# A three-layer mixed model on one core: the instruction order laid out by the scheduler's timeline machine model instead of its plain one

## The chip, the cores and the metric

The kernel runs on one core of a Trainium2 chip. Its engines are TensorE (PE, with its weight loads shown as PEld), VectorE (DVE), ScalarE (ACT), GpSimd (POOL) and SyncE (SP), which issues the loads. The metric is the device time in microseconds from start to end of one execution.

## The reference

The input is one sequence of 256 tokens of width 1024. Two blocks follow each other. The first has two layers, each with a feed-forward part, a mixer of three kinds of heads, a cross attention over 256 memory tokens, and a second feed-forward part. The second block is one hybrid layer with attention, a two-way gated delta rule and a convolutional feed-forward part. Cut to what matters:

```python
for l in range(2):                                            # first block
    x = x + 0.5 * swiglu(rms_norm(x, ...), ffn1_w_in[l], ffn1_w_out[l])
    z = rms_norm(x, ...) @ mix_w_in[l]                        # fox | moba | rwkv7
    x = x + concat([fox_mixer(..), rwkv7_mixer(..), moba_mixer(..)]) @ mix_w_out[l]
    x = x + memory_cross_attention(rms_norm(x, ..), rms_norm(mem, ..), ...)
    x = x + 0.5 * swiglu(rms_norm(x, ...), ffn2_w_in[l], ffn2_w_out[l])
# rwkv7_mixer, per token:   sa = S @ -kk
#   S = S * w + outer(sa, kk * a) + outer(v, k);   y = S @ r
mod = silu(c) @ w_mod + b_mod                                 # second block
ak, av, qkv, db, da, aq, z, gate = split_cols(modulate(rms_norm_2(x), sh1, sc1) @ w_in)
attn = latent_attention(q_x, [k_c, k_x], [v_c, v_x])
# gated delta rule: S_t = a_t (I - beta_t k_t k_t^T) S_(t-1) + beta_t k_t v_t^T;  o_t = S_t^T q_t
x = x + g1 * merge_branches(attn, gdn_output(gdn_bidirectional(ctx, x), z), gate)
x = x + g2 * conv_ffn(modulate(rms_norm_2(x), sh2, sc2), w_up, ..., w_down)
return rms_norm_2(x, final_norm_w)
```

The recurrences of `rwkv7_mixer` and of the gated delta rule are the serial parts. The kernel computes both in chunks, with the inverse of a unit triangular matrix in each chunk.

## The kernel before

**GEMMs.** Every product with a weight matrix is done in three passes with the operands split in a high and a low part, xh·wh + xl·wh + xh·wl. `piece` loads 128 x 1024 weights (512 KB) into `raw` (L370, SP's queue, 4 buffers), ACT makes `wh` (L319, 3 buffers) and DVE makes `wl` from both (L322, 3 buffers). The matmuls are L346, the transposes L349. `gemm_tok` has 512 columns per matmul (`wh`, `wl` as the moving operand), `gemm_chan` 256 columns (`xTh`, `xTl` as the moving operand, or `wh` stationary).

**Chains.** The rwkv heads of each mixer (function `rwkv`) run in two groups of heads, `gi` 0 and 1, and the gated delta rule of block 2 (`gdn`) in four groups. Each group builds a triangular matrix (`rN` in the mixers, L1121 and L1130; `gN` in block 2) and calls `inverse`: 15 stream shuffles (L696), 15 steps of a product `iv_p` (L322) and a sum `iv_x` (L343) on DVE, then the mask product (`rW`, or `xv` and `iv_tz` in block 2), transposes on DVE (L715, L735) and small matmuls on PE (`iv_tz,rN`, `rW,iv_tz`, `iv_tz,gN`) that double the size of the inverted blocks from 8 to 64 or 128. Behind it come the scans over the chunks (`rvt,rG`, `rX,rW`, `rSB` in a mixer; `gS,gQD`, `gdl,kT` in block 2) and the evacuation into `ry`, `rzr` or `go`. In the cross attention `xq` is the query, `xP` the softmax numerator and `macc` the product of the modulation weights with the condition vector, done on DVE (L340) out of raw weight pieces and summed over partitions by 128 x 2 matmuls.

**Order.** The functions are Python generators. `run` steps a main generator and merges side work into it by times (`Side`, `START`, `PACE`, the numbers given to `yield`), which fixes the order in which the instructions are traced. The tile layer then schedules them: it takes the traced instructions of all engines, goes through them greedily on a model of the machine, and lays out one order for each engine and the semaphore waits between the engines. On the chip every engine takes its instructions in that order. SP issues the loads in order too, and a load into `raw` waits until the splits of the piece four before have read it.

```python
r = s.stage.tile([128, 1024], F32, name="raw", bufs=4)         # raw
s.nc.sync.dma_start(r[:, :n], src)
h = s.stage.tile([128, 1024], F32R, name="wh", bufs=3)         # piece
l = s.stage.tile([128, 1024], F32R, name="wl", bufs=3)
s.act(h[:, :n], r[:, :n])
s.sub(l[:, :n], r[:, :n], h[:, :n].bitcast(F32))
```

The scheduler is chosen where `kernel` opens the tile context (L2054); all instructions come from `body`.

## Time and profile before

| | |
|---|---|
| median of 3 runs | 2138.4 us (2137.61 to 2144.73) |
| the profiled execution | 2140.43 us, span 2138.6 us |
| mean granted TensorE clock | 0.967 |
| PE, DVE, ACT, POOL busy | 96%, 75%, 53%, 1% |
| moved by DMA | 317.18 MB, 148 GB/s in the mean |

The stages, as the timeline shows them: feed-forward 0 to 235 us, mixer 0 to 447, cross attention 0 to 505, two feed-forward parts with the context side of block 2 beside them to 1040, mixer 1 to 1250, cross attention 1 with the modulation beside it to 1310, feed-forward to 1500, block 2's delta rule and attention to 1830, and the rest of block 2 to the end.

The page lists busy time, slices of the span, queues, the chain of work that ended last and the costliest groups. A matmul's end is modelled, so two of them overlap in the list, and what PE needs for one is read from the distance between starts. [...]

### The profile page before, as it was taken

How to read it: one execution, taken by the hardware profiler on the slowest of the kernel's cores; microseconds unless marked ns; L12 is line 12 of the kernel's file. 1: busy time of each engine (PE TensorE's matmuls, PEld its weight loads, DVE VectorE, ACT ScalarE, POOL GpSimd, SP SyncE). 2: the span in 40 equal slices, each digit the busy share in tenths (PEclk: the TensorE clock that was granted, in tenths of full speed). 3: DMA queues.
4: the chain of work that ended last, by engine and by line, in shares of the span. 5: the costliest groups of instructions: out<-in, count | busy, mean ns of one | idle time of the engine just before them, and what ended most of it. 6: DMA issues, size and time to landing. Idle time of an engine off the chain costs nothing.

```text
span 2138.6 us, 37333 instructions
## 1 busy us (share of the span) xinstructions
PE 2049.2 (96%) x14344; PEld 1808.0 (85%) x14344; DVE 1603.7 (75%) x3832; ACT 1131.0 (53%) x2113; POOL 14.9 (1%) x16
## 2 busy tenths in 40 slices
PE   8999999999999999999999979999889999999998
PEld 8899887778989989898888758889678888878996
DVE  6888688477686959586688576777778787767985
ACT  6544555376455555454555455435545565546663
POOL 0000000000000000000000000000000000000000
PEclk9999999899999999999999889999978999999999
DMA  7777432154554545454432154776431123555664
GB/s 246 226 236 231 154 110 70 52 169 131 166 160 140 156 139 159 137 166 145 148 107 80 53 187 155 248 239 206 138 99 60 40 70 93 168 165 167 194 192 128
DMA packets 90571, 317.18 MB, mean 148 GB/s; under 512 B 10389, under 2 KB 12953, under 8 KB 90009
## 3 DMA queue, kind: packets, MB, share of 16 engines
q1 hardware_dynamic: 90392, 314.80, 46.7%
q8 instruction: 112, 1.84, 0.3%
q14 instruction: 67, 0.54, 0.1%
HBM read 313.72 MB, written 1.05 MB: 147 GB/s over the span
## 4 chain that ended last, share of the span: by engine, by line
PE 73%; DVE 16%; DMA 5%; ACT 4%; issue 2%; SPq 0%; DVEq 0%; ACTq 0%
PE b L346 69%; DVE wl L322 4%; DMA raw<-in_wmod_dram 4%; PE b L349 3%; ACT wh L319 1%; DVE iv_x L343 1%; DVE iv_tz L696 1%; DVE macc L340 1%; DVE iv_p L322 1%; DVE gcv L340 1%; ACT sq L319 1%; DVE sg L322 1%; ACT iv_c L319 0%; DVE sg L340 0%; DVE iv_tz L322 0%
## 5 line engine op out<-in xcount | busy, mean ns | idle before, releaser
L319 ACT ACTIVATE wh<-raw 128x1024 fp32r<-128x1024 f32 (+1 forms) x546 | 568.6, 1042 | 553.9 <-PE b L346 437.9
L322 DVE TENSOR_TENSOR wl<-raw,wh 128x1024 fp32r<-128x1024 f32 (+1 forms) x546 | 653.8, 1203 | 242.9 <-ACT wh L319 211.5
L346 PE MATMUL b<-xTh,wh 128*128 128x256 f32 x2200 | 626.8, 286 | 2.8 <-ACT xTh L319 2.4
L346 PE MATMUL b<-xTh,wl 128*128 128x256 f32 x2200 | 622.4, 283 | 7.3 <-DVE wl L322 5.8
L346 PE MATMUL b<-xTl,wh 128*128 128x256 f32 x2200 | 621.8, 283 | 0.2 <-DVE xTl L340 0.2
L346 PEld LDWEIGHTS b<-xTh,wl 128*128 128x128 f32 x2200 | 418.4, 190 | 10.9 <-DVE wl L322 7.7
L346 PEld LDWEIGHTS b<-xTh,wh 128*128 128x128 f32 x2200 | 417.2, 190 | 8.5 <-ACT xTh L319 4.4
L346 PEld LDWEIGHTS b<-xTl,wh 128*128 128x128 f32 x2200 | 418.4, 190 | 2.7 <-DVE xTl L340 0.8
L346 PE MATMUL b<-wh,gh 128*128 128x512 f32 x440 | 177.7, 404 | 2.4 <-DVE x L340 2.2
L346 PE MATMUL b<-wl,gh 128*128 128x512 f32 x440 | 174.4, 396 | 0.2 <-DVE wl L322 0.2
L346 PE MATMUL b<-wh,gl 128*128 128x512 f32 x440 | 174.0, 396 | 0.0
L346 PE MATMUL b<-wh,xTh 128*128 128x512 f32 x400 | 163.6, 414 | 6.4 <-DVE iv_x L343 5.0
L346 PE MATMUL b<-wl,xTh 128*128 128x512 f32 x400 | 164.2, 412 | 0.3 <-DVE wl L322 0.3
L346 PE MATMUL b<-wh,xTl 128*128 128x512 f32 x400 | 161.4, 404 | 0.0
L340 DVE SCALAR_TENSOR_TENSOR macc<-raw,mcs,macc 128x512 f32<-128x512 f32 x112 | 82.4, 746 | 31.9 <-DMA raw<-in_wmod_dram 31.6
L346 PEld LDWEIGHTS b<-wh,gh 128*128 128x128 f32 x440 | 83.7, 190 | 20.8 <-DVE x L340 2.9
L346 PEld LDWEIGHTS b<-wl,gh 128*128 128x128 f32 x440 | 83.7, 190 | 19.6 <-DVE wl L322 0.6
L346 PEld LDWEIGHTS b<-wh,xTh 128*128 128x128 f32 x400 | 76.4, 192 | 26.2 <-issue 9.1
L346 PEld LDWEIGHTS b<-wh,gl 128*128 128x128 f32 x440 | 83.8, 191 | 17.0
L346 PEld LDWEIGHTS b<-wl,xTh 128*128 128x128 f32 x400 | 76.5, 191 | 20.1 <-issue 3.7
L346 PEld LDWEIGHTS b<-wh,xTl 128*128 128x128 f32 x400 | 76.9, 192 | 15.5 <-issue 1.0
L319 ACT ACTIVATE iv_tz<-b 32x128 f32<-32x128 f32 (+2 forms) x96 | 31.1, 324 | 63.5 <-PE b L346 62.5
(608 smaller groups left out, 3189.7 us busy)
## 6 DMA issues: line engine op xcount, KB each, us to landing
raw<-in_f1i_dram SPq DMA_DIRECT2D x88, 512.0 KB, 4.4
raw<-in_f2i_dram SPq DMA_DIRECT2D x88, 512.0 KB, 3.8
raw<-in_wmod_dram SPq DMA_DIRECT2D x48, 512.0 KB, 4.3
raw<-in_wup_dram SPq DMA_DIRECT2D x44, 512.0 KB, 4.3
raw<-in_f1o_dram SPq DMA_DIRECT2D x40, 512.0 KB, 4.1
raw<-in_wi_q_dram SPq DMA_DIRECT2D x40, 512.0 KB, 3.8
raw<-in_f2o_dram SPq DMA_DIRECT2D x40, 512.0 KB, 4.0
raw<-in_wi_a_dram SPq DMA_DIRECT2D x32, 512.0 KB, 3.9
```

What stands on the lines that cost most here:

```text
L319: return s.nc.scalar.activation(out, in_, func, scale=scale, bias=bias, **kw)
L322: return s.nc.vector.tensor_tensor(out, a, b, op=op)
L340: return s.nc.vector.scalar_tensor_tensor(out, a, sc, b, op0=op0, op1=op1)
L343: s.nc.vector.tensor_reduce(out, in_, axis=AX.X, op=op)
L346: s.last_mm = s.nc.tensor.matmul(out, lhsT, rhs, start=start, stop=stop).ins
L349: s.nc.tensor.transpose(out, in_, s.c("ident"))
L696: nc.vector.stream_shuffle(AR[:, j, :, j:], NC[:, :, j:], [j] * 16 + [16 + j] * 16)
```

## The change

One argument is added. The scheduler then goes through the same traced instructions on its timeline model of the machine instead of the plain one. All instructions stay, by name and operands, but for two more ACT table loads (6 instead of 4); what changes is their order on each engine and, with it, the waits. The orders of PE (11000 rows before, 11002 now) differ in 7227 lines, those of DVE in 5602, of ACT in 2160, of SP in 88; POOL's is the same.

```diff
-    with tile.TileContext(nc) as tc:
+    with tile.TileContext(nc, schedule_with_timeline_sim=True) as tc:
         body(tc, d, out)
```

Three places. The number behind a tile's name is that of the tile, so that a row can be found on both sides.

First, PE where the second inverse of mixer 0 (`iv_tz_3967` with `rN_3645`) begins, before:

```order
L346 MATMUL b4_4066<-rX_4056,rW_2996 128x64 x4
L346 MATMUL b1_4152<-wh_4253,xTh_71 128x512
L346 MATMUL b1_4152<-wh_4253,xTl_72 128x512
L346 MATMUL b2_3999<-iv_tz_3967,rN_3645 128x64 x4
L346 MATMUL b4_4097<-rE_3110,ra_3109 128x128
L346 MATMUL b3_4005<-iv_tz_3967,rN_3645 128x64 x4
L346 MATMUL b2_4021<-iv_tz_3967,rW_3722 128x64 x4
L346 MATMUL b3_4027<-iv_tz_3967,rW_3722 128x64 x4
L346 MATMUL b4_4097<-rE_3110,rzk_3134 128x256
```

and now:

```order
L346 MATMUL b6_4039<-PT_3986,fmv_2839 64x128 x8
L346 MATMUL b4_4185<-rE_3110,ra_3109 128x128
L346 MATMUL b4_4185<-rE_3110,rzk_3134 128x256
L349 MATMUL b7_4413<-fconst_67,qk_4064 128x128 x4
L346 MATMUL b2_3999<-iv_tz_3967,rN_3645 128x64 x4
L346 MATMUL b3_4005<-iv_tz_3967,rN_3645 128x64 x4
L349 MATMUL b6_4419<-fconst_67,qk_4064 128x128 x4
L346 MATMUL b0_4461<-wh_4467,xTh_71 128x512
L346 MATMUL b1_4462<-wh_4467,xTh_71 128x512
```

Before, the inverse's first three groups stand close together, with two GEMM matmuls (`wh_4253`) ahead of them and single products of `rE_3110` between. Now two transposes of `qk` stand around its first groups, and GEMM matmuls of a later piece (`wh_4467`) come ahead of the group with `rW_3722`. Up to its first row 1920 GEMM matmuls of the kernel stand ahead, against 1904 before; up to `b5_4330`, the product `rvt,rG` behind the inverse, 1944 against 1943.

Second, PE where the fourth inverse of block 2 (`iv_tz_19313` with `gN_18915`) begins, before:

```order
L346 MATMUL b1_19433<-wl_19502,xTh_71 128x512
L346 MATMUL b0_19434<-wh_19501,xTh_71 128x512
L346 MATMUL b2_19349<-iv_tz_19313,gN_18915 128x64 x4
L346 MATMUL b3_19343<-iv_tz_19313,gN_18915 128x64 x4
L346 MATMUL b0_19434<-wh_19501,xTl_72 128x512
L346 MATMUL b2_19379<-iv_tz_19313,xv_19027 128x64 x3
L346 MATMUL b3_19373<-iv_tz_19313,xv_19027 128x64 x4
L346 MATMUL b2_19379<-iv_tz_19313,xv_19027 128x64
L346 MATMUL b0_19434<-wl_19502,xTh_71 128x512
L346 MATMUL b0_19434<-wh_19501,xTh_71 128x512
```

and now:

```order
L346 MATMUL b1_19833<-wl_19874,xTh_71 128x512
L349 MATMUL b4_19572<-fconst_67,ggam_16382 128x128 x4
L346 MATMUL b2_19349<-iv_tz_19313,gN_18915 128x64 x4
L346 MATMUL b3_19343<-iv_tz_19313,gN_18915 128x64 x4
L346 MATMUL b2_19379<-iv_tz_19313,xv_19027 128x64 x4
L346 MATMUL b3_19373<-iv_tz_19313,xv_19027 128x64 x4
L346 MATMUL b3_19409<-iv_tz_19313,gN_18915 32x32 x4
L346 MATMUL b2_19415<-iv_tz_19313,gN_18915 32x32 x4
L346 MATMUL b3_19421<-iv_tz_19313,gN_18915 32x32 x4
L346 MATMUL b2_19427<-iv_tz_19313,gN_18915 32x32 x4
```

Before, GEMM matmuls stand between the inverse's groups. Now the inverse stands in one piece of 80 matmuls, and 8274 GEMM matmuls of the kernel stand ahead of it, against 8131 before. The transposes of `go` behind it stand at 8406, against 8448.

Third, ACT in cross attention 1, where `xq` is evacuated, before:

```order
L319 ACTIVATE wh_13784<-raw_13782 128x1024
L319 ACTIVATE xTh_71<-b3_13715,prm_69 128x256 x2
L319 ACTIVATE xq_13800<-b1_13686,nr_13728 128x512
L319 ACTIVATE sq_13803<-xq_13800 128x512
L319 ACTIVATE xq_13800<-b2_13687,nr_13728 128x512
L319 ACTIVATE sq_13807<-xq_13800 128x512
L319 ACTIVATE xqT_13818<-b4_13819,prm_69 128x512
L319 ACTIVATE xqT_13818<-b5_13825,prm_69 128x512
L319 ACTIVATE wh_13960<-raw_13958 128x1024
L319 ACTIVATE wh_13978<-raw_13976 128x1024
L319 ACTIVATE wh_14004<-raw_14002 128x1024
```

and now:

```order
L319 ACTIVATE wh_13784<-raw_13782 128x1024
L319 ACTIVATE wh_13960<-raw_13958 128x1024
L319 ACTIVATE wh_13978<-raw_13976 128x1024
L319 ACTIVATE wh_14004<-raw_14002 128x1024
L319 ACTIVATE xq_13800<-b1_13686,nr_13728 128x512
L319 ACTIVATE xq_13800<-b2_13687,nr_13728 128x512
L319 ACTIVATE sq_13803<-xq_13800 128x512
L319 ACTIVATE xqT_13818<-b4_13819,prm_69 128x512
L319 ACTIVATE xqT_13818<-b5_13825,prm_69 128x512
L319 ACTIVATE sq_13807<-xq_13800 128x512
```

Before, one piece is split ahead of `xq_13800` and three (13960, 13978, 14004) behind `xqT_13818`; now all four stand ahead of `xq_13800`.

## Rows read from the trace of the kernel before

**Rows 1.** The page: busy by engine, GB/s by slice, chain, weight splits on DVE.

```profile
PE 2049.2 (96%) x14344; PEld 1808.0 (85%) x14344; DVE 1603.7 (75%) x3832; ACT 1131.0 (53%) x2113; POOL 14.9 (1%) x16
...
GB/s 246 226 236 231 154 110 70 52 169 131 166 160 140 156 139 159 137 166 145 148 107 80 53 187 155 248 239 206 138 99 60 40 70 93 168 165 167 194 192 128
...
PE 73%; DVE 16%; DMA 5%; ACT 4%; issue 2%; SPq 0%; DVEq 0%; ACTq 0%
...
L322 DVE TENSOR_TENSOR wl<-raw,wh 128x1024 fp32r<-128x1024 f32 (+1 forms) x546 | 653.8, 1203 | 242.9 <-ACT wh L319 211.5
```

**Rows 2.** Windows: stretch, length, busy and count (PE, PEld, DVE, ACT, POOL), PEclk, DMA, GB/s.

```profile
235.00:447.00 212.00, 206.56 (x1422) 165.61 (x1421) 152.23 (x457) 107.51 (x238) 6.25 (x5) 0.95 0.31 98
329.00:363.40 34.40, 34.34 (x239) 27.01 (x239) 30.66 (x104) 19.94 (x51) 1.39 (x1) 1.00 0.26 81
375.00:394.00 19.00, 19.00 (x117) 13.14 (x116) 2.38 (x5) 4.02 (x10) 1.38 (x1) 0.51 0.09 28
505.00:1040.00 535.00, 523.72 (x4076) 485.24 (x4075) 401.26 (x954) 283.87 (x531) 1.39 (x2) 0.98 0.49 151
1040.00:1250.00 210.00, 205.87 (x1445) 165.72 (x1443) 158.83 (x469) 111.18 (x247) 5.96 (x5) 0.97 0.31 98
1500.00:1793.00 293.00, 270.45 (x1936) 239.03 (x1935) 236.26 (x820) 162.63 (x375) 0.00 (x0) 0.91 0.27 82
1950.00:2000.00 50.00, 50.00 (x442) 50.00 (x442) 42.39 (x70) 34.01 (x53) 0.00 (x0) 1.00 0.57 179
```

**Rows 3.** Timeline of PE, mixer 0: start, us, engine, line, operation, out<-in, count, idle.

```profile
366.91 1.00 PE L346 MATMUL b<-iv_tz,rN 128*128 128x64 f32 x8
...
388.64 1.97 PE L346 MATMUL b<-rW,iv_tz 64*64 64x64 f32 x16
...
408.04 1.00 PE L346 MATMUL b<-rvt,rG 128*128 128x64 f32 x8
...
417.06 1.10 PE L346 MATMUL b<-rX,rW 128*128 128x64 f32 x8
...
446.79 0.39 PE L346 MATMUL b<-wh,xTl 128*128 128x512 f32 x1
447.02 0.40 PE L346 MATMUL b<-wl,xTh 128*128 128x512 f32 x1
```

**Rows 4.** Waits of the whole span: who for whom, us in total, times, longest.

```profile
ACT wh L319 <- PE b L346: 437.9, 343, 5.4
...
ACT wh L319 <- DMA raw<-in_f1i_dram: 17.2, 10, 2.8
...
PE b L346 <- DVE iv_tz L322: 9.4, 6, 2.7
```

**Rows 5.** Timeline of ACT at the start: split of the fifth piece, a table load.

```profile
19.19 1.06 ACT L319 ACTIVATE wh<-raw 128x1024 fp32r<-128x1024 f32 x1 [1.72 <-PE b L346]
...
32.83 1.28 ACT L319 ACT_TABLE_LOAD   x1
```

**Rows 6.** Timeline of DVE, mixer 0: the mask product that opens the second inverse.

```profile
363.43 2.17 DVE L322 TENSOR_TENSOR rW<-iv_x,fconst 128x512 f32<-128x512 f32 x2
```

**Rows 7.** Timeline of ACT and PE in cross attention 1, idle time and releaser in brackets.

```profile
1258.43 0.69 ACT L319 ACTIVATE xq<-b,nr 128x512 f32<-128x512 f32 x1 [4.58 <-DVE nr L340]
...
1267.37 1.06 ACT L319 ACTIVATE wh<-raw 128x1024 fp32r<-128x1024 f32 x1 [1.41 <-DMA raw<-in_xo_dram]
...
1270.67 1.87 PE L346 MATMUL b<-fconst,macc 128*128 128x2 f32 x8 [6.82 <-DVE macc L340]
...
1272.90 0.56 ACT L319 ACTIVATE xP<-b,at_mxx,xrq 128x256 f32<-128x256 f32 x1 [4.48 <-DVE at_mxx L340]
```

**Rows 8.** Timeline of PE in block 2: fourth inverse, its last scan product, transposes of go.

```profile
1795.01 2.00 PE L346 MATMUL b<-iv_tz,gN 128*128 128x64 f32 x16 [0.83 <-DVE iv_tz L322]
...
1828.47 0.39 PE L346 MATMUL b<-gdl,kT 128*128 128x128 f32 x2
...
1886.90 1.47 PE L349 MATMUL b<-fconst,go 128*128 128x128 f32 x12
```

## The prediction

> **What bounds the kernel now.** I read the page first, then the windows by stage, then the waits, then the timelines of the four places where PE loses time. The page says that PE is busy for 96% of the span and that the chain which ends last runs 73% through PE, 16% through DVE [rows 1]. That busy time is modelled, so it cannot be taken as "PE at its peak". Starts are better. In the feed-forward part 442 matmuls start in 50 us, one every 0.113 us for 256 columns [rows 2], and in a mixer's tail two neighbouring 512-column matmuls start 0.23 us apart [rows 3]. Against these two steps the stages split in two kinds. The feed-forward stages (1950 to 2000 us is a sample) run at the step, and no order can help there. The others are chains: the 64-column blocks of the two mixers (235 to 447 and 1040 to 1250 us), the second cross attention (1250 to 1310), and block 2's gated delta rule (1500 to 1887). [...] In these chains PE steps through small matmuls, each waiting for an evacuation or a DVE step, and weight GEMMs are the filler between them. ACT's largest wait is 437.9 us for PE to free a weight buffer, so weight pieces are ready ahead of PE nearly everywhere, and PE's own named waits are small (9.4 us on the largest, DVE's iv_tz) [rows 4]. So the time sits in the order of PE and DVE around the chains, which is exactly what this change rewrites.
>
> **What the change does.** No instruction comes or goes but two more ACT table loads, 1.28 us each [rows 5] on an engine that is idle 47% of the span [rows 1], so I cost them at nothing; if all of their time fell on a chain, 2.6 us. The orders show one pattern in all chain stages: GEMMs and weight splits are pulled ahead of chain steps, and chain steps then stand in long runs with no GEMM between them. The longest such run on PE was 54 matmuls before; now there are runs of 136 and 82 (mixer 0), 116 and 112 (mixer 1), 57 (end of the context side), 132, 140 and 80 (block 2). Six terms follow.
>
> **Start: +1.** The rest of fconst, prm, pos and mem, 1.94 MB, now stand on SP's queue right after the fourth weight piece instead of being spread up to the tenth. With the x tiles and the four pieces that is 5.1 MB ahead of the fifth piece; at the 246 GB/s of the first slices [rows 1] it has landed at about 21 us, the fifth piece 2 us later. Before the change the fifth piece was split at 19.2 us, and what came last there was a buffer that PE freed [rows 5]. So a shift of up to 4 us is possible, and PE has 24 matmuls of each piece to work off against it. ACT waited 17.2 us in all for these pieces [rows 4]. Bounds 0 and +5; I take +1, since later pieces then come sooner than before.
>
> **Mixer 0: -10.** In the order, 36 DVE instructions now stand ahead of the mask product rW that opens the second inverse (rope and norm steps of fox and moba, three rG copies, two splits) and none went behind it. With each one's own time from the trace they are 10.2 us. DVE was idle for 3.7 of the 34.4 us ahead of that rW, which starts at 363.4 [rows 2, 6], so rW comes at about 370 (+6.5). On PE the second inverse starts at 366.9, ends at 390.5, and the product rvt,rG of its scan came only at 408.0 [rows 3], because 36 GEMMs and the tail of the first scan stood between. Now 1932 GEMMs instead of 1907 stand ahead of the inverse's end, and only 12 behind it up to rvt,rG. So that product comes about 4 us after the inverse's end at 396, near 400, which is 8 us earlier. From there rX,rW came 9.0 us later (417.06) and the last GEMM at 447.0 [rows 3], of which the last 41 GEMMs (9.5 us at 0.23) ran bare behind the chain; now 24 stand there (5.5 us), 48 having moved up between the scan steps, which costs each of these steps 1 to 3 us. Chain to about 431.5, then 24 GEMMs: end near 437, not 447. Bounds: -16 if DVE takes the 36 instructions wholly in its gaps, +2 if all 10.2 us are on the path and the 32 GEMMs of lost cover (7.4 us) are paid. I take -10.
>
> **Mixer 1: -8.** The same code with 1445 matmuls in 210 us against 1422 in 212 [rows 2]; DVE work ahead of its rW is 8.4 us more, and the bare runs are a little shorter. Bounds -13 and +2.
>
> **Cross attention 1: +4.** Now ACT splits three pieces of in_xo before it evacuates xq. The third of these waited for its DMA until 1267.4, while xq ran at 1258.4 [rows 7]; ACT runs in order, so xq moves to about 1267. Before, PE then stood 6.82 us for macc [rows 7]; that macc is now made ahead of the chain, so this wait pays most of the shift back. From xq at 1267 on: transposes, scores, two reduces and the reciprocal-root steps end near 1276.5, where xP was evacuated at 1272.9 [rows 7]. Bounds +2 (the DMA is issued 2 to 3 us earlier) and +8 (nothing of the wait paid back). Taken: +4.
>
> **Block 2's delta rule: -10.** This is the largest moved block. Before, the fourth inverse starts at 1795.0, its last scan product ends at 1828.5, and the transposes of go stand at 1886.9, behind 252 GEMMs that ran bare [rows 8]. That is 91.9 us, of which 317 GEMMs at 0.23 are 73. Now 143 of these GEMMs (33 us) and 12 splits (14.4 us at 1203 ns [rows 1]) stand ahead of the inverse, the inverse is an 80-matmul run, and 84 GEMMs cover the step from scan to go. From the inverse's start: about 32 us to the scan (as now), 23 us to go (the 84 GEMMs, 19.3 us, fit in), 42 more GEMMs, 9.7 us: about 66 us for what took 92, so -26, if the inverse still starts at 1795. It starts later by what the 33 us of GEMMs and 14.4 us of splits don't find room for. In 1500 to 1793 DVE is idle for 56.7 of 293 us and PE starts only 1936 matmuls at clock 0.91 [rows 2]. So there is room, but in pieces, between chain steps that PE takes in order. Ends: 0 and +33. I take half, +16, nearest to the idle time that DVE shows, which is long enough but is itself made of waits for PE. So -10, bounds -26 and +7.
>
> **Context side and the rest: -1.** In 505 to 1040 us PE is busy for 523.7 of 535 [rows 2]. The waits for iv_tz there go, 9 us or so. At the end a bare run of 57 stands in front of mixer 1, some 10 us. Taken 0, bounds -8 and +8. Cross attention 0 has a bare run of 28 (+1), the stretch behind the delta rule some more GEMMs ahead (-2).
>
> **Sum.** +1 -10 -8 +4 -10 -1 = -24. The profiled execution took 2140.43 us, so 2116.4; it lies 2.0 us above the median of the runs, 2138.4, so the forecast is **2114.5**.
>
> **A rule against the change.** Row first: in the stretch with the sparsest PE work the granted clock was 0.51, and it is 1.00 where GEMMs stand densely [rows 2]. [...]
>
> **The rivals.** (1) Slower: the bare runs cost more than the filler gains. Place: the eight new runs. At clock 0.51 a matmul of such a run takes 0.162 us (19 us over 117 [rows 2]), and a GEMM that falls into it takes twice its 0.23. If the GEMMs pulled ahead find no gap there, they push the chain back by their length and then miss as cover. That gives the upper bounds: mixers +2 each, block 2 +7, context +8, cross attention +8, start +5, total +32, or 2170; two thirds of it, as likely as not all six at once, 2160. It decides from the point where the fourth inverse starts more than 26 us later than 1795. For it: 855 matmuls in bare runs, the clock of 375 to 394. Against it: in these chains PE waits for DVE and ACT, and a slow clock on 32-column matmuls costs little when the next step is late anyway. (2) No change: DVE's extra work delays each chain by what the denser tail returns, mixers -2 each, block 2 0, the other terms as taken (+1 +4 -1): 0, or 2138. For it: PE is "busy" 96% and 73% of the last chain. (3) More: DVE and PE take the filler wholly in gaps, mixers -16 and -13, block 2 -26, rest +4: -51, or 2087. For it: 56.7 us of DVE idle in one stretch. The order does change on all engines, so that the change does nothing at all is ruled out.
>
> **How the numbers follow.** The forecast case (2100 to 2131) gets 0.42, the larger gain (under 2100) 0.19, no change (2131 to 2146) 0.19, slower (above) 0.20. A measurement of this kernel can tell about 0.3%, 6.4 us, from no change: 2132 and 2145 are its edges. Faster is 0.42 + 0.19 and a little of the third case, 0.62; same 0.17; slower 0.21. The range leaves out a tenth on each side: from 2084, just under rival 3, to 2156, just under rival 1.
>
> **What would show it.** In the profile of the changed kernel: mixer 0's second rW near 370 and its rvt,rG near 400, no bare block of 41 GEMMs at its end, and the end near 437; the clock may still read about 0.5 there. Cross attention 1 with no 6.8 us wait for macc, but xP 4 us further behind mixer 1's last GEMM than before. Block 2: about 66 us, not 92, from the fourth inverse's first matmul to the GEMM that before stood behind the transposes of go, and that first matmul no more than 16 us late against what was won earlier. The feed-forward stages keep 442 matmuls in 50 us. I am wrong if a chain start moves by the full length of the GEMMs placed ahead of it, or if PE in the bare runs is seen waiting at a step that used to be hidden (macc, xq, gN).

## The result and the profile after

| | before | after |
|---|---|---|
| median | 2138.0 us (2135.35 to 2144.73, 4 runs) | 2223.6 us (2220.44 to 2226.45, 4 runs) |
| ratio, 95% interval | | 1.0392, 1.0354 to 1.0430 |
| span of the profiled execution | 2138.6 us | 2224.7 us |
| mean granted clock | 0.967 | 0.941 |

The kernel became 3.9% slower. The forecast was 2114.5 with a range from 2084 to 2156, so the sign was wrong and the time lies 68 us above the range.

From the page of the changed kernel: busy time by engine, the clock by slice (against the GB/s row of [rows 1], for place), and two groups with their idle time and its releaser.

```profile
PE 2078.8 (93%) x14344; PEld 1838.3 (83%) x14344; DVE 1614.2 (73%) x3832; ACT 1130.3 (51%) x2115; POOL 14.9 (1%) x16
...
PEclk9999998689999999999898788999999999899999
...
L322 DVE TENSOR_TENSOR wl<-raw,wh 128x1024 fp32r<-128x1024 f32 (+1 forms) x546 | 653.6, 1200 | 267.2 <-ACT wh L319 254.9
...
L340 DVE SCALAR_TENSOR_TENSOR macc<-raw,mcs,macc 128x512 f32<-128x512 f32 x112 | 82.2, 748 | 58.4 <-DMA raw<-in_wmod_dram 57.9
```

The same work is done (DVE's splits take 653.6 us, as in [rows 1]); PE stands for 146 us instead of 89, its busy time grew from 2049 to 2079 us, and the clock is low in slices 7 to 9 (mixer 0; a slice is 55.6 us) and 22 to 25 (mixer 1).

To see where the 86 us arise, the starts of equal weight matmuls are compared: the k-th of the 9960 weight matmuls of one trace with the k-th of the other (for 8563 of them the operands' names are the same on both sides, the others are swapped with near ones). The lag of the changed kernel grows like this:

| stage (weight matmuls) | forecast | measured | lag at its end |
|---|---|---|---|
| start (to 600) | +1 | +1.5 | 1.5 |
| feed-forward 1 (to 1440) | 0 | +10.9 | 12.4 |
| mixer 0 (to 2015) | -10 | +25.5 | 37.9 |
| cross attention 0 (to 2280) | +1 | +7.9 | 45.8 |
| middle feed-forward with the context side (to 5310) | 0 | -12.8 | 33.0 |
| mixer 1 (to 5940) | -8 | +30.9 | 63.9 |
| cross attention 1 (to 6060) | +4 | +3.1 | 67.0 |
| feed-forward (to 7440) | 0 | +6.8 | 73.8 |
| block 2 to the end | -12 | +11.2 | 85.0 |

Each trace is one execution, and the same order came out up to 9 us apart in a stage (last section), so terms of a few us are not told from that. The two mixers are 56 of the 85 us. The windows there, after (length, busy and count of PE, PEld, DVE, ACT, POOL, then clock, DMA share, GB/s); the last is the sample of the dense part behind block 2:

```profile
335.00:368.00 33.00, 31.98 (x269) 24.88 (x267) 24.56 (x48) 17.46 (x41) 0.95 (x1) 1.00 0.32 98
368.00:405.00 37.00, 31.66 (x176) 25.12 (x175) 28.33 (x113) 12.92 (x37) 2.76 (x2) 0.68 0.01 2
405.00:442.00 37.00, 37.00 (x218) 26.46 (x217) 16.39 (x44) 14.32 (x43) 0.00 (x0) 0.58 0.06 19
...
2036.00:2086.00 50.00, 50.00 (x444) 50.00 (x443) 41.42 (x68) 34.16 (x53) 0.00 (x0) 1.00 0.57 181
```

From 368 to 442 us the granted clock is 0.63 in the mean (0.68 and 0.58 in the two halves above) and almost nothing is loaded (2 and 19 GB/s). Before, it was 0.86 over the same 74 us, with 0.51 in 19 of them (375 to 394, [rows 2]). Counting the `wh` matmuls alone (two of every three weight matmuls) shows what is missing; the rows are before, then after, 365 to 435 us (PE busy and count of these, clock, DMA share, GB/s):

```profile
365.00:435.00 70.00, 17.36 (x47) 0.85 0.13 41
```

```profile
365.00:435.00 70.00, 3.70 (x8) 0.66 0.06 18
```

In the same 70 us 47 of them started before, and now 8. The stretch is not the same part of the chains on the two sides: before, it holds the second group's inverse and scan, now the first group's scan and the second group's inverse. The longest stretch without a weight matmul, 361.6 to 404.6 us, lies ahead of the second inverse, where the first group's scan runs; a second one fills most of the inverse (414.3 to 437.1 us). The steps of the prediction, on DVE and PE (to be read against [rows 6] and [rows 3]), with two weight matmuls in the half at clock 0.58, which start 0.42 us apart where two of [rows 3] start 0.23 apart:

```profile
398.62 2.09 DVE L322 TENSOR_TENSOR rW<-iv_x,fconst 128x512 f32<-128x512 f32 x2
...
402.54 1.67 PE L346 MATMUL b<-iv_tz,rN 128*128 128x64 f32 x14
...
434.20 1.97 PE L346 MATMUL b<-rW,iv_tz 64*64 64x64 f32 x16
...
439.88 0.63 PE L346 MATMUL b<-wh,xTh 128*128 128x512 f32 x1
440.30 0.63 PE L346 MATMUL b<-wh,xTl 128*128 128x512 f32 x1
...
442.20 1.00 PE L346 MATMUL b<-rvt,rG 128*128 128x64 f32 x8
...
460.80 1.00 PE L346 MATMUL b<-rX,rW 128*128 128x64 f32 x8
...
484.90 0.40 PE L346 MATMUL b<-wl,xTh 128*128 128x512 f32 x1
```

The second inverse itself, from its first matmul to its last, before and then after (windows as above):

```profile
366.90:390.60 23.70, 23.70 (x184) 17.77 (x182) 6.46 (x12) 5.56 (x16) 1.38 (x1) 0.63 0.03 4
```

```profile
402.54:436.17 33.63, 33.63 (x222) 24.39 (x222) 15.94 (x43) 11.05 (x31) 0.00 (x0) 0.63 0.07 21
```

The clock is 0.63 in both. The inverse's own 144 matmuls are the same; around them 78 others stand now, most of them small products of the other heads (`qkT`, `zg`, `gf`, `rE`), where 40 stood before.

### The profile page after: what moved, and what is told of

It is laid out like the page before. It is cut to its first block, busy times and chain, and to the rows that moved or that the text cites. A ratio compares the mean times of both kernels' runs of the same rounds, so it can differ in the third digit from the quotient of the medians.

```text
span 2224.7 us, 37374 instructions
## 1 busy us (share of the span) xinstructions
PE 2078.8 (93%) x14344; PEld 1838.3 (83%) x14344; DVE 1614.2 (73%) x3832; ACT 1130.3 (51%) x2115; POOL 14.9 (1%) x16
## 5 line engine op out<-in xcount | busy, mean ns | idle before, releaser
L322 DVE TENSOR_TENSOR wl<-raw,wh 128x1024 fp32r<-128x1024 f32 (+1 forms) x546 | 653.6, 1200 | 267.2 <-ACT wh L319 254.9
L346 PE MATMUL b<-xTh,wh 128*128 128x256 f32 x2200 | 620.4, 283 | 8.1 <-ACT xTh L319 4.9
L346 PE MATMUL b<-wl,gh 128*128 128x512 f32 x440 | 166.6, 399 | 1.9 <-DVE wl L322 1.9
L319 ACT ACTIVATE gh<-sg 128x256 fp32r<-128x256 f32 x88 | 35.9, 409 | 59.4 <-DVE sg L322 59.4
```

Source lines behind the costliest of these rows:

```text
L319: return s.nc.scalar.activation(out, in_, func, scale=scale, bias=bias, **kw)
L322: return s.nc.vector.tensor_tensor(out, a, b, op=op)
L346: s.last_mm = s.nc.tensor.matmul(out, lhsT, rhs, start=start, stop=stop).ins
```

## The experiments

Three theories stood at the start. **Filler first**: engines take their instructions in order, the new order has ready GEMMs and splits ahead of chain steps, so each chain comes later by their length. **Cold clock**: the loss is PE at the low granted clock in the runs without GEMMs (0.68 and 0.58 above). **DVE alone**: DVE's order is at fault, PE's is not. A fourth, **bare runs**, came out of the first eight kernels: the loss is made by long runs on PE without a weight matmul.

Most kernels hold a part of the program in the order of the other scheduler. The body is traced and scheduled once only to read that order; in the second tracing each held instruction gets an edge to the one that it follows there, an edge of issue order that adds no wait (cut to what matters):

```diff
+    first, _ = build(arrays, FROM)                 # order read from this one
     with tile.TileContext(nc, schedule_with_timeline_sim=BASE) as tc:
         body(tc, d, out, mark)
+        for eng, names in order.items():
+            last = None
+            for n in names:
+                if n in stage and eng in PINS.get(stage[n][0], ()):
+                    if last is not None:
+                        tc.add_manual_dep(stage[n][1], last, why, reason="order")
+                    last = n
```

| kernel | median, us | ratio to before, 95% interval |
|---|---|---|
| x1_mixers_plain | 2188.4 | 1.0215, 1.0162 to 1.0269 |
| x2_mixers_pe | 2209.7 | 1.0337, 1.0280 to 1.0394 |
| x3_mixers_dve | 2257.3 | 1.0541, 1.0491 to 1.0591 |
| x4_warm | 2252.7 | 1.0518, 1.0444 to 1.0592 |
| x5_mid_only | 2128.2 | 0.9939, 0.9917 to 0.9961 |
| x6_later_8 | 2152.5 | 1.0051, 1.0029 to 1.0073 |
| x7_later_16 | 2144.2 | 1.0004, 0.9982 to 1.0026 |
| x8_block2_plain | 2202.1 | 1.0293, 1.0261 to 1.0326 |
| x9_macc_late | 2214.0 | 1.0311, 1.0290 to 1.0332 |
| x10_mixers_pe_dve | 2188.8 | 1.0205, 1.0167 to 1.0243 |
| x11_warm_half | 2246.5 | 1.0456, 1.0389 to 1.0522 |
| x12_later_32 | 2167.8 | 1.0108, 1.0023 to 1.0193 |

The kernel before took 2137 to 2147 us beside them, so ratios are compared. The changed kernel's own is 1.0392, 1.0354 to 1.0430.

**Which engine's order (x1, x2, x3, x10).** `BASE` is the timeline scheduler, `FROM` the plain one, `ALL` stands for all five engines:

```diff
+PINS = {'mixer0': ALL, 'mixer1': ALL}                  # x1
+PINS = {'mixer0': ('PE',), 'mixer1': ('PE',)}          # x2
+PINS = {'mixer0': ('DVE',), 'mixer1': ('DVE',)}        # x3
+PINS = {'mixer0': ('PE', 'DVE'), 'mixer1': ('PE', 'DVE')}  # x10
```

> The timeline order everywhere but in the two mixers, where all engines keep the order of the plain scheduler. Filler first (in-order engines take ready GEMMs and splits ahead of chain steps, so each chain step comes later and its tail runs bare): both mixers go back to their length of before, and the lag of the changed kernel against the kernel before, which grew by 25 us in mixer 0 and by 22 us in mixer 1, no longer grows there; about 2223.6 - 47 = 2177 us. [...] If the loss sits in neither mixer's own order but in what is left from the stage ahead: above 2200.

> As the run with both mixers in plain order, but PE alone keeps the plain order there, DVE, ACT and SP stay free for the timeline scheduler. Filler first on PE (the GEMMs ahead of rN, of the first inverse and of the scan are what delays the chain): most of the 47 us come back, 2177 to 2190. Filler first on DVE (splits and norm steps between the steps of the first inverse delay it by 20 us or more): little comes back, 2205 to 2225.

> DVE alone keeps the plain order in both mixers. If DVE's order is the cause: 2177 to 2190. If PE's is: 2205 to 2225, since the first inverse may then start its DVE steps early but its PE steps stand behind the same GEMMs.

> The timeline order, with PE and DVE, and only these two, in plain order in both mixers. PE alone gave back 14 us of the run's 35, DVE alone made it 34 us slower. If the loss lies in how PE's and DVE's orders fit together: like the run with all engines in plain order, 2185 to 2195. If ACT's and SP's orders carry a part of their own: 2200 to 2212.

With all engines in plain order the mixers give 35 us back, less than the 47 expected, and mixer 0 runs step by step as before: from the sums of its first inverse on, every chain step lies 16.3 to 17.0 us behind its time before ([rows 3]), of which 13.1 us are the lag with which the stage begins. So the loss of the mixers is their order's. It can't be put down to one engine. PE alone returns 14 us (12 by the ratios, and its interval overlaps with the changed kernel's); DVE alone makes it 34 us worse; the two together (x10) return as much as all five (1.0205 and 1.0215), so no part of ACT's and SP's orders shows. The windows of mixer 0 and what follows, first x2, then x3 (235 to 500 us):

```profile
235.00:500.00 265.00, 243.26 (x1574) 194.39 (x1573) 181.93 (x513) 130.68 (x285) 7.31 (x6) 0.94 0.30 100
```

```profile
235.00:500.00 265.00, 240.97 (x1497) 192.53 (x1496) 162.02 (x482) 119.88 (x262) 7.31 (x6) 0.86 0.27 90
```

With PE's order held and DVE's free, PE stands (21.7 of 265 us) at a clock of 0.94; with DVE's held and PE's free it stands more (24.0 us) and the clock falls too, to 0.86. DVE alone is out as a theory, and so is "PE alone". What the two orders cost here is a matter of the pair; their single prices don't add up to it.

**Is the chain's late start the price (x6, x7)?** Plain scheduler, one edit in `rwkv`, where `inv` begins (8.0 in x6, 16.0 in x7):

```diff
             if gi:
                 yield "inv0"
+            else:
+                yield 8.0
             N = t([128, 8, 128], "rN")
```

> The plain scheduler everywhere. The only edit: the first group's triangular matrix and inverse are traced 8 units later in both mixers, so that on PE the first inverse stands behind 52 more GEMMs in mixer 0 (1820 for 1768) and 56 more in mixer 1; the timeline order had 116 and 124 more. Filler first: each GEMM ahead of the chain moves the chain by its own 0.23 us, and the tail is bare by as much; 108 GEMMs are 25 us, and at the 47 us that 240 GEMMs cost in the changed kernel 21 us: 2155 to 2162. If it is not the place of the chain but something else in the timeline order (the mixture on DVE, the places of loads): within 8 us of 2137.

> As the run with 8 units, but 16: the first inverse stands behind 104 more GEMMs in mixer 0 (1872) and 114 more in mixer 1 (5762), nearly as in the timeline order, but by the plain scheduler. Filler first: 218 GEMMs are 50 us at 0.23, 43 us by the rate of the changed kernel: 2175 to 2187, twice the rise of the run with 8. If GEMMs ahead find room in gaps and only the rest of the timeline order costs: 2137 to 2150.

Filler first, as it was stated, falls here. In x7 the second triangular matrix of mixer 0 comes at 356.6 us instead of 327.8, as late against the stage's start as in the changed kernel, and the whole kernel takes the time of before. x6 costs 11 us, less than expected, and twice its dose costs nothing; what x6 pays for stays open. The reading taken here is that a chain may start late as long as weight matmuls are left to stand between its later steps: x7 has 56 `wh` matmuls from 365 to 435 us, at a clock of 0.90. Two rows of x7 limit it. Its profile is the slowest of its ten executions, and there mixer 0 is 8 us and mixer 1 8 us longer than before; and the clock is low earlier, 0.52 from 326 to 365 us, while its first inverse runs.

```profile
365.00:435.00 70.00, 23.05 (x56) 0.90 0.18 56
```

```profile
326.00:365.00 39.00, 38.52 (x221) 29.58 (x221) 15.46 (x30) 11.27 (x36) 0.95 (x1) 0.52 0.13 41
```

**Bare runs (x12).** The same edit with 32.0, which leaves no weight matmul for the chains: one run of 161 chain matmuls in each mixer.

> The plain scheduler everywhere, with the one edit of the runs with 8 and 16, now 32 units: in each mixer the two chains end up together behind the last GEMMs that are ready, in one run of 161 matmuls on PE with no GEMM between them, where the changed kernel has runs of 136 and 82 (mixer 0), 116 and 112 (mixer 1), the kernel before none above 54, and the run with 16 none above 67. Bare runs (a long run without GEMMs brings the granted clock down to its lower level, PE itself becomes the bound there, and no GEMM is left to use the time): mixer 0 and mixer 1 20 to 30 us longer each, a clock near 0.6 for 40 to 60 us in each, 2180 to 2200. If a late chain costs as little as with 16 (whose time was that of before): 2140 to 2155, and the loss of the changed kernel lies in something that only the timeline order has.

It costs 23 us by the ratio, below the 40 to 60 expected and far above what 16 units cost, though by no scheduler but the plain one. In the profiled execution, which is 7 us above the median, mixer 0 is 21 us longer than before (25 in the changed kernel), with the same picture:

```profile
365.00:435.00 70.00, 8.09 (x18) 0.70 0.06 18
```

So long runs without weight matmuls are enough to lose time, under the plain scheduler too. The interval is wide (5 to 41 us), and mixer 1 lost 18 us where the changed kernel lost 31; what makes the rest there no run shows.

**The clock's share (x4, x11).** The order of the changed kernel, kept on every engine, and matmuls added whose results are overwritten (two at each bank in x4, one in x11; one copy makes their operand at the start; cut to what matters):

```diff
     def bank(s):
         s.i += 1
-        return s.b.bank(s.banks[s.i % len(s.banks)])
+        ps = s.b.bank(s.banks[s.i % len(s.banks)])
+        for _ in range(WARM if s.hot else 0):
+            s.b.mm(ps, s.b.wt[:, :128], s.b.wt)
+        return ps
```

> The order of the changed kernel on PE, DVE and SP, kept instruction by instruction, with 164 added matmuls of 512 columns, two at each PSUM bank that the second group's inverse and scan take in the mixers; their results are overwritten by the chain's own product, so they only keep PE at work in the bare runs. At 0.23 us each they are 38 us of PE time, at the slower clock level twice that. Cold clock: PE stands at 0.58 to 0.68 in the 74 us of mixer 0 from 368 to 442 us; with the added matmuls it stays near 1.0 and the chain steps get shorter, the mixers 10 to 15 us each, 2195 to 2205. Filler first, the clock being a sign and not the cause: the added matmuls gain nothing where each step waits for DVE or ACT and cost up to their own 38 us: 2224 to 2262.

> The order of the changed kernel with one added matmul at each bank, 82 in all, where the run with two had 164. That run brought the granted clock of mixer 0 between 368 and 442 us from 0.58 to 0.68 up to 0.91 to 0.95, and the mixer was as long as before. If the slow clock is the price of the bare runs (PE's own work at half speed) and the added matmuls ate what a full clock gave: with half of them a part is left over, mixer 0 is 4 to 10 us shorter and the whole 2205 to 2218. If the bare runs wait for the chain's steps on DVE and ACT whatever the clock is: mixer 0 as long as in the changed kernel, the whole 2222 to 2238.

x4 is slower than the changed kernel and x11's interval overlaps with that one's, so added work is no remedy. x4's 2252.7 lies in the range that its expectation gave to the other theory (2224 to 2262, the slow clock a sign and not the cause). x11's 2246.5 lies in neither of its ranges, and by its ratio, as 2235, in that of the other theory too (2222 to 2238). The whole times thus speak against the gain of 10 to 15 us in each mixer that a full clock was to bring. What follows is read from one profile of each kernel, after the fact: mixer 0, where the first group's scan and the second group's inverse lie at about 368 to 442 us in all three. After, x11, x4:

```profile
368.00:442.00 74.00, 68.66 (x392) 51.58 (x391) 44.73 (x157) 27.24 (x79) 2.76 (x2) 0.63 0.04 11
```

```profile
368.00:442.00 74.00, 69.42 (x363) 48.02 (x360) 40.48 (x149) 20.50 (x60) 2.81 (x3) 0.65 0.03 11
```

```profile
368.00:442.00 74.00, 69.77 (x472) 49.61 (x469) 45.97 (x158) 28.66 (x81) 2.87 (x3) 0.93 0.03 11
```

Against before, mixer 0 (weight matmuls 1320 to 2112) is 24.9 us longer with none added, 40.3 with 41 and 24.7 with 82. In x11's profile the clock stayed at 0.65 and the 41 cost 15.4 us, 0.38 each, which is more than 0.23 over 0.65: PE itself was the bound there, it didn't wait for late steps. In x4's the clock was 0.93 and the 82, 19 us at 0.23 each, came for nothing. So about 19 of the 25 us would be the slow clock, an estimate from these profiles. That the dose made the clock is not shown: x11's four executions lie between 2228 and 2258 us at mean clocks of 0.951 to 0.935, x4's between 2235 and 2263 at 0.956 to 0.942, and the profile of x11 is one of its two longer executions, that of x4 one of its two shorter. In mixer 1 the clock rose little (0.66 to 0.70 in 1230 to 1270 us) and the 82 cost 16 us.

That PE is the bound in the bare part of the inverse can also be read in the changed kernel. From 398 to 437 us it is the others that wait for PE, ACT for 8.1 us in front of `iv_tz`, DVE for 4.49 at one step:

```profile
ACT iv_tz L319 <- PE b L346: 8.1, 6, 5.7
```

```profile
429.17 0.28 DVE L758 COPY iv_tz<-b 32x128 f32<-32x128 f32 x1 [4.49 <-PE b L346]
```

Ahead of it, in the first group's scan, PE does stand: 5.3 of the 37 us from 368 to 405.

A second measure needs no edit. Each execution has its span and mean clock; span times (1 - clock) is its clock deficit. Over the 121 executions of these kernels that are on record with a clock, each set against the mean of its own kernel, the span rises by 0.82 us for each us of deficit (correlation 0.93). From the profiled execution before to the one after the deficit went from 71 to 131 us. If the slope held from one order to another, that would be 49 of the 86 us. No run shows that it does: x7's mean deficit is 10 us above that of the kernel before, at the same time. The page splits the 86 otherwise, 30 us of PE's busy time and 56 of its standing. How much of the whole loss is clock stays an estimate.

**Single stages (x8, x9, x5).** Timeline scheduler with block 2 in plain order; timeline scheduler with `macc` alone held on DVE in the first feed-forward part; plain scheduler with the middle stage in timeline order:

```diff
+BASE, FROM, PINS = True, False, {'block2': ALL}     # x8
+BASE, FROM, PINS = True, False, {'ffn1_0': ('DVE',)}   # x9, edges for macc only
+BASE, FROM, PINS = False, True, {'ffn_mid': ALL}    # x5
```

> The timeline order everywhere but in block 2, where all engines keep the plain order. The lag of the changed kernel grew by 11 us over block 2, in the three runs with edits in the mixers by 6 to 20. If that is block 2's own order: 2223.6 - 11 = 2212 us (2204 to 2218), and the fourth inverse starts 73 us later than before instead of 103. If block 2's order is a gain, as the prediction had it (-10): about 2233.

> The timeline order, but in the first feed-forward part each macc on DVE (the modulation weights times the condition vector) is held behind the instruction that it follows in the plain order; nothing else is held. In the changed kernel this stage is 13 us longer, DVE waits 57.9 us for the loads of wmod in front of macc (31.6 before), and PE stands 5.8 us at 123.9 us. If macc's place is the cause (DVE takes its instructions in order, and what stands behind macc waits for the load of wmod too): the stage goes back to within 3 us of before, 2212 us. If the loads themselves come late because of SP's order, or something else in the stage costs: no change, 2219 to 2226.

> The plain order everywhere but in the middle stage (second feed-forward part of layer 0, first of layer 1, with the context side), which keeps the timeline order on all engines. In the four kernels with the timeline order there so far the lag against the kernel before fell by 11 to 13 us over this stage. If that gain is the stage's own: 2137 - 11 = 2126 us (2122 to 2130). If it is only a loss of the stages ahead that is paid back there (loads that ran ahead while PE was late): 2135 to 2140.

x8: block 2's order is a loss, 11.7 us in the profile (the lag grows by 11.2 over block 2 in the changed kernel and falls by 0.5 in x8) and some 21 by the medians (more than expected). The fourth inverse and the transposes of `go` are each 73.0 us behind [rows 8]:

```profile
1867.99 1.22 PE L346 MATMUL b<-iv_tz,gN 128*128 128x64 f32 x9 [0.83 <-DVE iv_tz L322]
...
1959.88 1.47 PE L349 MATMUL b<-fconst,go 128*128 128x128 f32 x12
```

x9: `macc` is the cause in the first feed-forward part. In the changed kernel DVE stood before a load of `wmod`, and the update of x, which needed nothing of it, stood behind it; PE then waited for x. DVE, then PE, after:

```profile
127.54 1.41 DVE L340 SCALAR_TENSOR_TENSOR macc<-raw,mcs,macc 128x512 f32<-128x512 f32 x2 [5.49 <-DMA raw<-in_wmod_dram]
128.87 0.74 DVE L340 SCALAR_TENSOR_TENSOR x<-b,r4f,x 128x512 f32<-128x512 f32 x1
```

```profile
129.67 0.79 PE L346 MATMUL b<-wh,gh 128*128 128x512 f32 x1 [5.38 <-DVE x L340]
```

With `macc` held back its waits up to 235 us fall from 19.6 to 6.0 us (us in total, times, longest; first after, then x9), and the stage (weight matmuls 0 to 1320) is 1.2 us longer than before instead of 13.4:

```profile
DVE macc L340 <- DMA raw<-in_wmod_dram: 19.6, 12, 5.5
```

```profile
DVE macc L340 <- DMA raw<-in_wmod_dram: 6.0, 5, 2.2
```

x5: the middle stage is the one where the timeline order wins, and the gain is its own. At 2128.2 us this version beats both kernels, 0.61% under the one before (interval 0.4 to 0.8%). In its profile the stage with its bare end is 14 us shorter, and 9 are lost again in mixer 0, at a clock of 0.74 in 40 us of it (below).

## Why the prediction was wrong, point by point

**Start, +1; cross attention 1, +4; the dense parts.** Right: 1.5 and 3.1 us, and 444 matmuls in 50 us. In the cross attention it went as described. `xq` moved to 1327.06, behind the third piece, and the wait for macc shrank, while one for xP came up (against [rows 7]; ACT, then PE):

```profile
1326.09 1.06 ACT L319 ACTIVATE wh<-raw 128x1024 fp32r<-128x1024 f32 x1 [1.44 <-DMA raw<-in_xo_dram]
1327.06 1.25 ACT L319 ACTIVATE xq<-b,nr 128x512 f32<-128x512 f32 x2
```

```profile
1327.52 1.84 PE L346 MATMUL b<-fconst,macc 128*128 128x2 f32 x8 [4.11 <-DVE macc L340]
1341.41 2.27 PE L349 MATMUL b<-fconst,xP 128*128 128x128 f32 x8 [7.40 <-DVE xP L335]
```

**Mixer 0, -10, and mixer 1, -8.** These two terms failed, by 36 and 39 us; mixer 1's was taken over from mixer 0's. Four steps of the working, in the stage's own time (12.4 us taken off):
- The second rW was put 6.5 us later, for 36 DVE instructions. It came 22.8 later. The first inverse stands behind 1884 weight matmuls instead of 1768 and starts 20 us later; the prediction looked only at the second (1920 against 1904).
- From the inverse's end to `rvt,rG` it said 4 us where there were 17: 6.0, nearly right, a gain of 11.
- The inverse itself was taken to keep its 23.7 us; it took 33.6, at the same clock of 0.63, with 222 matmuls started in it instead of 184; and from `rvt,rG` to the second `rX,rW` 18.6 us instead of 9.0 (1 to 3 us for each step had been allowed).
- The end was read as "less bare", because 24 weight matmuls stand behind the chain instead of 41. The tail did get shorter, by 6 us. But the bare stretch had moved to the middle, 136 and 82 matmuls with hardly a weight matmul between. The working priced lost cover there only in the bound (7.4 us) and the slow clock not at all.

x7's times show that the first of these need not be a loss. The fourth is one: x12 has the long bare run without the timeline order. The third stands in no run alone. The sentence that failed is the one against the first rival, "a slow clock on 32-column matmuls costs little when the next step is late anyway". In the inverse the next step wasn't late: PE was busy for 37.00 of 37.00 us at 0.58, and ACT and DVE waited for it.

**The row set against the change** pointed the right way: the clock was 0.51 in the sparsest stretch and 1.00 where GEMMs stand densely [rows 2], and nothing of that is in the sum. The clock did fall: 0.63 over 74 us in mixer 0 (368 to 442), where before it was 0.86 (before):

```profile
368.00:442.00 74.00, 73.61 (x458) 52.76 (x459) 36.66 (x106) 29.80 (x71) 1.38 (x1) 0.86 0.17 53
```

"Sparsest" is right of the count of matmuls only (117 in 19 us), not of PE's listed busy time: 19.00 of 19.00 us at 0.51 there [rows 2], and 37.00 of 37.00 at 0.58 after (405 to 442). What stands in both is a run of small matmuls with few weight matmuls between (7 of the `wh` matmuls in the 19 us, 16 in the 37).

**Block 2, -10.** The fourth inverse starts 29 us later against the stage's start, where +16 had been taken and 33 was the bound: the GEMMs ahead of it pushed it by nearly their whole length. From it to the weight matmul behind `go` it took 76 us; 66 had been said, 93.5 it was. So -26 became -18 and +16 became +29, together +11. x8 confirms the sign.

```profile
1898.10 2.52 PE L346 MATMUL b<-iv_tz,gN 128*128 128x64 f32 x16 [1.72 <-DVE iv_tz L322]
...
1962.38 1.36 PE L349 MATMUL b<-fconst,go 128*128 128x128 f32 x11
```

**Context side, 0.** -12.8, beyond its bound of -8: the waits for iv_tz that were named did go, and what the bare end took back was less than they gave. Where the rest of the 12.8 comes from stays open.

**Not in the sum**: `macc` in the first feed-forward part (+10.9). The prediction put the feed-forward stages at nothing because "no order can help there"; an order can hurt there, and it had the wait for `macc` only in cross attention 1. Two more rises were missing, that of cross attention 0 (+7.9 for +1) and that of the last feed-forward part (+6.8), where `macc` is also done beside it, but that wasn't tried. What costs 7 us in cross attention 0 stays open.

**The rivals.** The first was right in kind, and its test decided right: the fourth inverse starts 29 us later, its point was 26. Its price, 2160 to 2170, was too low by more than 50 us, since it was built from bounds (+2 for a mixer) that held neither PE's speed in a bare run nor its standing.

## What to carry to other kernels

When an order changes, don't look only at what stands ahead of a chain's start: count the independent matmuls left for each of its later steps, to its end. A chain that starts late (x7, ratio 1.0004) cost nothing that the times show while such matmuls lasted. In the changed kernel, where they ran out, the clock fell (0.58 from 405 to 442 us), PE became the bound (busy for all 37 us), and its matmuls took nearly twice as long (0.42 us from start to start, for 0.23); filling the runs with useless ones gave no time back (x4 1.0518, x11 1.0456, for 1.0392). Work on an in-order engine that waits for a load belongs behind what doesn't need it (x9: the stage 1.2 us longer than before instead of 13.4), and a new order is best tried stage by stage, on all engines of the stage together: here one of eight stages gained. Count, too, what stands inside a serial step: the inverse got 10 us longer (33.6 for 23.7) at an unchanged clock of 0.63, with 38 more matmuls of the other heads in it (counted, not tried by itself).

## What the runs showed of the hardware

The same order can be granted another clock. In x5 the orders of PE, DVE and ACT up to the end of mixer 0 are those of before, and up to weight matmul 1760 the two traces stay 1.3 us apart; then x5's clock is 0.74 in the mean of 300 to 340 us, and by weight matmul 1800 it has fallen back by 8.7 us. Before, then x5:

```profile
300.00:340.00 40.00, 38.30 (x380) 34.57 (x380) 33.17 (x100) 23.89 (x55) 0.95 (x1) 1.00 0.28 92
```

```profile
300.00:340.00 40.00, 38.31 (x310) 34.43 (x309) 24.64 (x57) 17.50 (x40) 0.95 (x1) 0.74 0.26 87
```

A busy share of 38.3 us in both hides it; the count of matmuls, 380 against 310, and the clock show it. Executions of one kernel differ here by 0.1% (x9's four) to 1.6% (x5's twelve), and their time goes with their clock (correlation 0.93 above), so a profile's stage should be compared with its clock beside it.
